# Sparse attention: the indexer's weighted sum on TensorE, the probabilities scaled on ScalarE, one rotation sum on GpSimd, and transfers traced by staging tile

## The chip, the cores and the metric

The kernel runs on one core of a Trainium2 chip. The metric is the device time of one execution in microseconds (us), as a median of runs. Engines are named as in the profile: PE is TensorE (PEld its weight loads), DVE is VectorE, ACT is ScalarE, POOL is GpSimd and SP is SyncE, whose queue starts the transfers.

## The reference, cut to what matters

A stack of six stages works on one sequence of 256 tokens with 1024 features: a state-space mixer (s5), an MLP (mlp0), sparse attention (dsa), an MLP (mlp1), a mixer of state-space and windowed attention (mix2) and a gated MLP (ffn2). Each stage but s5 is a few large products with weight matrices that are read from memory once. The change touches the sparse attention and the end of s5, and how the weights are fetched everywhere. The attention, shortened:

```
proj = h @ w_in
q, k, v, qi, ki, wi = split(proj); q, k, qi, ki = apply_rope(...)
wi = wi * (IDX_HEADS ** -0.5 * IDX_DIM ** -0.5)              # 8 indexer heads
rel = relu(einsum('bthd,bsd->bths', qi_blk, ki))
score = einsum('bths,bth->bts', rel, wi_blk)                 # sum over the 8 heads
score = where(causal, score, -inf)
_, idx = top_k(score, 64)
att = einsum('btngd,btknd->btngk', qg, kg) * scale           # only the chosen keys
p = softmax(where(valid, att, -inf))
o = einsum('btngk,btknd->btngd', p, vg)
out = o @ w_out
```

`apply_rope` is `x * cos + rot(x) * sin`: two products and a sum.

## The kernel before

All activations stay in SBUF in two halves of 128 tokens, h=0 and h=1. Every weight matrix is cut into units of 128 x 1024 fp32 (512 KB). `plan` writes down the order of all units of the whole kernel beforehand. `fetch` starts the transfer of a unit into a staging tile, `raw`, of which there are four. `send` calls `fetch` if that is still to be done and splits the unit into a high part `wh` (a cast on ACT, L162) and a low part `wl` (a subtraction shared by DVE and POOL, L165); the products then take three matmuls for each pair of operands (hi x hi, hi x lo, lo x hi, L223 and L233). `pump` calls `send` while there is a free pair of `wh` and `wl` tiles, `consumed` gives such a pair back. The splits have a lower priority than what is traced around them.

The order of the instructions on each engine is set when the program is built, by a scheduler that takes, of the instructions that it believes ready, the one traced first. On the chip each engine then works its list in order. The kernel helps with a clock of its own: `clock[0]` counts the estimated time of PE, `after(delay, fn)` puts a piece of work off, `tick` runs what is due, `need` forces it.

Stage s5 ends with a product of two halves (L710); `pump` is called just before it (L705), at a point with room for nine units (four in one pool, five in another). `fin(h, acc)` then normalises a half: squares on ACT (`act_squares`, L252), products with the gain on DVE (L309), a power on POOL (L257), the update of `x` (L312), and the same again for the next stage's norm (`pre_norm`), whose `dg` (L284) lets PE turn the half (L291) and start the next stage.

Stage dsa projects the indexer's columns and k, v for each half, then q in two chunks of heads. `idx_T` turns the indexer's queries and keys, `scores` multiplies them (L771), `rel` is the relu on ACT (L777), and DVE sums the eight heads with their weights `wis` (L784 for the first, L786 for seven more), 128 keys wide for h=0 and 256 for h=1. `topk` then runs eight rounds of max and replace on DVE and leaves `bias[h]`. `rope` runs on DVE (L718, L721, L722). `att(h, n)` treats four heads: scores (L867), masked scores with their maximum on DVE (L873), exponentials with their sum on ACT (L877), a reciprocal and the scaling of the four rows on DVE (L878, L880), then `turn_P` (transposes on PE, L887, copies on ACT, L890) and `pv` (L897). There are eight such calls; while they run, PE has the projection of q's second chunk and, once the heads are there, the product with `w_out` to do.

Of the kernel before, what the change touches and what calls it, by code (L numbers as in the profile page):

```python
# [11 lines left out]
F32 = mybir.dt.float32  # L12
# [30 lines left out]
INIT = 3  # L43
WARM = 12
# [6 lines left out]
def kernel(ctx: ExitStack, tc: tile.TileContext, d: dict, out: bass.AP, stages=None):  # L51
# [8 lines left out]
    raw_p = ctx.enter_context(tc.tile_pool(name="raw", bufs=4))  # L60
# [61 lines left out]
    stream = {"plan": [], "at": 0, "units": [], "sent": 0, "got": 0, "done": 0}  # L122
# [20 lines left out]

    def send():
        unit = stream["units"][stream["sent"]]
# [8 lines left out]
        raw = unit[6] if len(unit) > 6 else fetch(unit)  # L154
# [11 lines left out]
        unit[1:3] = [t[:, :tot].rearrange("p (k n) -> p k n", n=n) for t in (hi, lo)]  # L166

# [82 lines left out]
    def act_squares(src, ss, i, scale=1.0 / 32):  # L250
        junk = nrm_p.tile([128, 512], BF16, tag="junk", name="junk", bufs=1)
        act.activation(junk, src[:, HALVES[i]], AF.Square, scale=scale, accum_out=ss[:, i:i + 1])  # L252
# [50 lines left out]
    def post_norm(h, acc, gain):  # L303
        ss = square_sums()
        ag = nrm_p.tile([128, DM], F32, tag="xs", name="ag")
        for i in range(2):
            act_squares(acc, ss, i)
        for cs in HALVES:
            dve.tensor_tensor(ag[:, cs], acc[:, cs], gain[:, cs], OP.mult)  # L309
        r = rstd_of(ss)  # L310
        for cs in HALVES:
            dve.scalar_tensor_tensor(x[:, h, cs], ag[:, cs], r, x[:, h, cs], OP.mult, OP.add)  # L312

# [66 lines left out]
    def s5(hook):  # L380
# [290 lines left out]
        for i in range(8):  # L671
# [44 lines left out]
    def rope(dst, tmp, src, cos, sin, nh):  # L716
# [5 lines left out]
        dve.tensor_tensor(dst, dst, tmp, OP.add)  # L722
# [12 lines left out]
    def dsa(hook):  # L735
# [10 lines left out]
        pj = sp.tile([128, 2, 584], F32, name="pj")  # L746
        wis = sp.tile([128, 2, 8], F32, name="wis")
        qiT = sp.tile([128, 2, 4, 128], F32, name="qiT")
# [8 lines left out]
        def idx_T(h, io):  # L757
            iof = io.rearrange("p n e -> p (n e)")
            act.copy(qiT[:, h], transposes(iof[:, :512]).rearrange("p (j t) -> p j t", t=128))
# [3 lines left out]
            sco = rp.tile([128, T], F32, tag="sco", name="sco")[:, :nk]  # L763

            def scores(j0):
                need(*[ti[i] for i in range(h)])
                pss = [mm_tile().rearrange("p (j s) -> p j s", s=nk) for _ in range(2)]
                for j in range(j0, j0 + per):
                    for e in range(2):
                        es = slice(e * 64, e * 64 + 64)  # L770
                        pe.matmul(pss[e][:, j - j0, :], qiT[es, h, j, :], kiT[es, :nk], start=True, stop=True,  # L771
# [15 lines left out]

            def topk(j0):
                scores(j0)
                bs = base[:, T - nk:]  # L790
                dve.scalar_tensor_tensor(sco, bs, 1e30, sco, OP.add, OP.add)
# [7 lines left out]
            if h == 0:  # L799
                tix[h] = after(1.5, lambda: topk(0))  # L800
            else:
                def first():
                    scores(0)
                    tix[h] = after(2.0, lambda: topk(2))
                tix[h] = after(1.5, first)
# [8 lines left out]
        def on_kv(h, ps):  # L814
# [5 lines left out]
            tk[h] = after(4.0, lambda: act.copy(  # L820
# [4 lines left out]
        for h in range(2):  # L825
            need(xready[h])
            for n in range(2):
                ps = mm_tile()
                tok_mms(ps[:, :292], xTh, xTl, h, units[n])
                act.copy(pj[:, h, 292 * n:292 * n + 292], ps[:, :292])  # L830
            dve.tensor_scalar(wis[:, h], pj[:, h, 576:584], 8 ** -0.5 * 64 ** -0.5, None, OP.mult)
            io = rp.tile([128, 10, 64], F32, tag="S", name="io")
            it = rp.tile([128, 9, 64], F32, tag="rt", name="it", bufs=1)
            rope(io[:, :9], it, heads(pj[:, h, :576]), cosr[:, h], sinr[:, h], 9)
# [19 lines left out]
        def att(h, n):  # L854
# [24 lines left out]
            for i in range(4):  # L879
                dve.tensor_scalar(S[:, i], S[:, i], den[:, i:i + 1], None, OP.mult)  # L880
# [25 lines left out]
            fins[h, n] = after(3.2 + nk * 0.011, turn_P)  # L906
# [584 lines left out]
    def fin(h, acc):  # L1491
        name, nxt = now["name"], now["next"]
        with tc.high_priority(URGENT):
            if name in post_g:
                post_norm(h, acc, now["post"])
# [4 lines left out]
            else:  # L1500
                nc.sync.dma_start(out[0, HS[h], :], x[:, h, :])

# [97 lines left out]
```

## Time and profile before

| | |
|---|---|
| median of 3 runs | 1251.39 us (1243.54 to 1251.98) |
| the profiled execution | 1247.13 us, its span 1245.3 us |
| PE busy | 1203.2 us, 97% of the span |
| DVE, ACT, POOL busy | 859.4, 666.4, 362.2 us |

A busy PE is not PE at its full rate: the granted clock, the column PEclk, is 1.00 over most of the span and falls to about a half in a few places. Times in the trace are microseconds from the start of the span. dsa's products run from about 286 us to 411 us; s5 ends, and mlp0 begins, at about 99 us. Columns of a window are, for each engine, busy time and number of instructions.

### The profile page before, as it was taken

The numbers are of one execution on the slowest core, as the hardware profiler recorded it, in microseconds if no ns is written. First come the engines' busy times: TensorE is split into PE (matmuls) and PEld (weight loads), VectorE is DVE, ScalarE is ACT, GpSimd is POOL, SyncE is SP. The second block draws the span as 40 slices with busy tenths as digits, with TensorE's granted clock in tenths as the row PEclk, the third lists the DMA queues.
The fourth block names the chain that finished last, engine by engine and source line by source line (L and its number), as shares of the span: only waits on it lengthen the run. The fifth ranks groups of instructions, "written<-read, shape, count | busy, mean of one in ns | idle before, by whom it ended". The sixth has DMA issues, their size and how long they took to land.

```text
span 1245.3 us, 20243 instructions
## 1 busy us (share of the span) xinstructions
PE 1203.2 (97%) x7462; PEld 1031.5 (83%) x7462; DVE 859.4 (69%) x1560; ACT 666.4 (54%) x1207; POOL 362.2 (29%) x355
## 2 busy tenths in 40 slices
PE   7799999999889999999999999999999999999998
PEld 4347998988656899998889989988999888899997
DVE  7978654547986866553788875886776557797662
ACT  7636554436556655443555655665555344855541
POOL 6840000025311545441132124300111004655540
PEclk8899999999879999999999999999999999999999
DMA  8126655536430665552654465444443455766630
GB/s 332 35 81 205 202 188 187 201 113 197 158 125 4 217 202 192 178 193 85 208 164 151 136 195 178 132 143 137 121 134 110 147 170 178 250 194 208 180 108 34
DMA packets 107987, 198.51 MB, mean 159 GB/s; under 512 B 7569, under 2 KB 52593, under 8 KB 107889
## 3 DMA queue, kind: packets, MB, share of 16 engines
q1 hardware_dynamic: 107889, 197.23, 49.8%
q8 instruction: 59, 0.97, 0.3%
q14 instruction: 39, 0.32, 0.1%
HBM read 196.15 MB, written 1.05 MB: 158 GB/s over the span
## 4 chain that ended last, share of the span: by engine, by line
PE 71%; issue 7%; DVE 7%; DMA 4%; ACT 3%; POOL 2%; SPq 0%; DVEq 0%; ACTq 0%; POOLq 0%
PE mm L233 27%; PE acc L223 20%; PE mm L223 14%; DVE wl L165 2%; PE mm L263 1%; DMA raw<-in_w_up_dram 1%; POOL wl L165 1%; DMA raw<-in_mlp_w_dram 1%; DVE xbc L1056 1%; ACT wh L162 1%; PE mm L291 1%; PE mm L897 1%; PE acc L867 1%; PE mm L1117 1%; POOL rstd L257 1%
## 5 line engine op out<-in xcount | busy, mean ns | idle before, releaser
L165 DVE TENSOR_TENSOR wl<-raw,wh 128x512 fp32r<-128x512 f32 (+5 forms) x477 | 414.4, 904 | 183.8 <-ACT wh L162 173.8
L162 ACT CAST wh<-raw 128x512 fp32r<-128x512 f32 (+2 forms) x477 | 364.9, 814 | 212.6 <-PE acc L223 112.4
L165 POOL TENSOR_TENSOR wl<-raw,wh 128x96 fp32r<-128x96 f32 (+3 forms) x252 | 249.7, 1012 | 409.3 <-ACT wh L162 371.5
L233 PE MATMUL mm<-xTh,wh 128*128 128x256 f32 x1056 | 303.5, 287 | 0.0
L233 PE MATMUL mm<-xTh,wl 128*128 128x256 f32 x1056 | 298.8, 283 | 0.0
L233 PE MATMUL mm<-xTl,wh 128*128 128x256 f32 x1056 | 298.6, 283 | 0.0
L233 PEld LDWEIGHTS mm<-xTh,wh 128*128 128x128 f32 x1056 | 201.7, 191 | 4.3 <-issue 2.7
L233 PEld LDWEIGHTS mm<-xTl,wh 128*128 128x128 f32 x1056 | 201.9, 191 | 1.0
L233 PEld LDWEIGHTS mm<-xTh,wl 128*128 128x128 f32 x1056 | 201.8, 191 | 0.0
L223 PE MATMUL mm<-wh,xTh 128*128 128x512 f32 (+2 forms) x384 | 146.4, 386 | 0.0
L223 PE MATMUL mm<-wl,xTh 128*128 128x512 f32 (+2 forms) x384 | 142.8, 376 | 0.0
L223 PE MATMUL acc<-wh,hh 128*128 128x512 f32 x344 | 106.3, 390 | 0.0
L223 PE MATMUL acc<-wl,hh 128*128 128x512 f32 x344 | 106.2, 390 | 0.0
L223 PE MATMUL mm<-wh,xTl 128*128 128x512 f32 (+2 forms) x384 | 102.2, 381 | 0.8 <-DVE xTl L117 0.8
L223 PE MATMUL acc<-wh,hl 128*128 128x512 f32 x344 | 87.5, 390 | 0.0
L223 PEld LDWEIGHTS mm<-wh,xTh 128*128 128x128 f32 x384 | 73.1, 190 | 13.0 <-ACT xTh L116 0.3
L223 PEld LDWEIGHTS mm<-wl,xTh 128*128 128x128 f32 x384 | 73.0, 190 | 11.9
L223 PEld LDWEIGHTS mm<-wh,xTl 128*128 128x128 f32 x384 | 68.2, 190 | 13.7 <-issue 1.3
L223 PEld LDWEIGHTS acc<-wl,hh 128*128 128x128 f32 x344 | 64.6, 188 | 13.8
L223 PEld LDWEIGHTS acc<-wh,hl 128*128 128x128 f32 x344 | 64.4, 188 | 13.4
L223 PEld LDWEIGHTS acc<-wh,hh 128*128 128x128 f32 x344 | 63.2, 188 | 12.1
L257 POOL TENSOR_TENSOR rstd<-ss,mhalf 128x1 f32<-128x1 f32 x18 | 12.9, 719 | 182.2 <-DVE ss L255 177.5
(379 smaller groups left out, 1647.0 us busy)
## 6 DMA issues: line engine op xcount, KB each, us to landing
raw<-in_mlp_w_dram SPq DMA_DIRECT2D x128, 512.0 KB, 4.5
raw<-in_w_in_dram SPq DMA_DIRECT2D x69, 512.0 KB, 4.2
raw<-in_w_up_dram SPq DMA_DIRECT2D x36, 512.0 KB, 4.4
raw<-in_w_in_dram SPq DMA_DIRECT2D x64, 256.0 KB, 4.4
raw<-in_w_down_dram SPq DMA_DIRECT2D x22, 512.0 KB, 4.4
raw<-in_w_ssd_proj_dram SPq DMA_DIRECT2D x16, 512.0 KB, 3.7
raw<-in_att_w_in_dram SPq DMA_DIRECT2D x12, 512.0 KB, 4.9
gain<-in_norm_g_dram SPq DMA_DIRECT2D x9, 512.0 KB, 5.3
```

The source lines that it names most:

```text
L162: act.copy(hi[:, cs], raw[:, cs])
L165: eng.tensor_tensor(lo[:, cs], raw[:, cs], hi[:, cs].bitcast(F32), OP.subtract)
L223: pe.matmul(dst[:, a:b], half(lhs, k0 + k, h), rhs[:, a:b], start=first and i == 0 and rhs is wh and not lo, stop=last and i == len(units) ...
L233: pe.matmul(dst.rearrange("p (h t) -> p h t", h=2), lhs[:, c0:c0 + 128], rhs[:, :, k, :], start=i == 0 and m == 0, stop=i == len(units) - ...
L257: pool.tensor_tensor(r, ss[:, 0:1], mhalf[:, 0:1], OP.pow)
L263: pe.transpose(tp[:, j * 128:(j + 1) * 128], src[:, j * 128:(j + 1) * 128], ident)
L291: pe.matmul(tp[:, j * 128:(j + 1) * 128], xg[:, (a + j) * 128:(a + j + 1) * 128], dg, start=True, stop=True)
L867: pe.matmul(aps[:, e, j, :nk], qT[es, h, 2 * n + j, :], kT[es, n, :nk], start=True, stop=True, tile_position=(e * 64, 0))
L897: pe.matmul(ops[e * 64:e * 64 + 64, :256].rearrange("p (j t) -> p j t", j=2), kv[:, s, 256 + n * 64:256 + n * 64 + 64], PT[:, :, e, :], st ...
L1056: dve.scalar_tensor_tensor(o[:, s:], ps[:, e, :T - s], cwb[:, 3 - s, ft:ft + 1], o[:, s:], OP.mult, OP.add)
L1117: pe.matmul(ops[es, :128], v[:, s, g, c0:c0 + 64], PTs[e][:, b * 128:(b + 1) * 128], start=b == 0, stop=b == nb - 1, tile_position=(0, e * ...
```

## The change

Five things are changed, and three of them are in dsa.

1. The sum over the indexer's heads moves to PE. For each half POOL builds `dgw`, eight 128 x 128 diagonal matrices with the heads' weights (one instruction of 128 x 1024). The new `weigh` multiplies each head's `rel` by its diagonal and accumulates all eight in one PSUM tile, `tot`; `topk` reads that. `weigh` is put off by 2.5 us after the scores.
2. In `att` the four scalings move from DVE to ACT (Identity with a scale for each row), and `turn_P` is put off by 1.8 us more.
3. The sum in `rope` for q moves from DVE to POOL, and q's transposes are put off by 7 us instead of 6, k's by 5 instead of 4.
4. `prefetch` traces the transfers of up to four units beyond the last one sent, each time a unit is sent, instead of with the unit's own split. The number of staging tiles stays four.
5. At the end of s5 only six units are sent ahead of the last product; the rest is sent after the first half's squares, and its ACT instructions are queued behind them.

`pj` and `qiT` lose the copy that they had for each half, which makes room for `dgw`.

```
+RAWS = 4
+FIRST = 6
...
-        return raw
+
+    def prefetch():
+        while stream["asked"] < min(stream["sent"] + RAWS, len(stream["units"])):
+            fetch(stream["units"][stream["asked"]])
+            stream["asked"] += 1
 
     def send():
+        prefetch()
         unit = stream["units"][stream["sent"]]
...
-        raw = unit[6] if len(unit) > 6 else fetch(unit)
+        raw = unit[6]
...
         unit[1:3] = [t[:, :tot].rearrange("p (k n) -> p k n", n=n) for t in (hi, lo)]
+        prefetch()
...
-                for unit in stream["units"][:4]:
-                    fetch(unit)
+                prefetch()
...
-        pump()
+        while stream["sent"] < FIRST:
+            send()
         for h in range(2):
...
-            fin(h, acc)
+            squared = fin(h, acc)
+            if h == 0:
+                with tc.issue_after(squared.ins):
+                    pump()
...
-    def rope(dst, tmp, src, cos, sin, nh):
+    def rope(dst, tmp, src, cos, sin, nh, adder=None):
...
-        dve.tensor_tensor(dst, dst, tmp, OP.add)
+        (adder or dve).tensor_tensor(dst, dst, tmp, OP.add)
...
+            dgw = rp.tile([128, 8, 128], F32, tag="dgw", name="dgw", bufs=1)
+            pool.tensor_tensor(dgw, ident[:, None, :].to_broadcast([128, 8, 128]),
+                               wis[:, h, :, None].to_broadcast([128, 8, 128]), OP.mult)
+            tot = []
...
+                tix[h] = after(2.5, lambda: weigh(j0, rels))
+
+            def weigh(j0, rels):
+                if not tot:
+                    tot.append(mm_tile()[:, :nk])
                 for j in range(j0, j0 + per):
                     for e in range(2):
                         hd = 2 * j + e
-                        w = wis[:, h, hd:hd + 1]
-                        if hd == 0:
-                            dve.tensor_scalar(sco, rels[e][:, j - j0], w, None, OP.mult)
-                        else:
-                            dve.scalar_tensor_tensor(sco, rels[e][:, j - j0], w, sco, OP.mult, OP.add)
+                        pe.matmul(tot[0], dgw[:, hd], rels[e][:, j - j0], start=hd == 0, stop=hd == 7)
+                clock[0] += per * 2 * nk * 0.00086
+                if j0 + per < 4:
+                    scores(j0 + per)
+                else:
+                    topk()
...
-                dve.scalar_tensor_tensor(sco, bs, 1e30, sco, OP.add, OP.add)
+                dve.scalar_tensor_tensor(sco, bs, 1e30, tot[0], OP.add, OP.add)
...
-            tk[h] = after(4.0, lambda: act.copy(
+            tk[h] = after(5.0, lambda: act.copy(
...
-                rope(qr, qt, heads(ps), cosr[:, h], sinr[:, h], 8)
-                tq[h, n] = after(6.0, lambda: act.copy(
+                rope(qr, qt, heads(ps), cosr[:, h], sinr[:, h], 8, pool)
+                tq[h, n] = after(7.0, lambda: act.copy(
...
-                dve.tensor_scalar(S[:, i], S[:, i], den[:, i:i + 1], None, OP.mult)
+                act.activation(S[:, i], S[:, i], AF.Identity, scale=den[:, i:i + 1])
...
-            fins[h, n] = after(3.2 + nk * 0.011, turn_P)
+            fins[h, n] = after(5.0 + nk * 0.011, turn_P)
```

## Rows read from the trace of the kernel before

**Rows 1.** The page, busy time of each engine over the span.

```profile
PE 1203.2 (97%) x7462; PEld 1031.5 (83%) x7462; DVE 859.4 (69%) x1560; ACT 666.4 (54%) x1207; POOL 362.2 (29%) x355
```

**Rows 2.** Waits of PE, whole span: total us, times, longest us.

```profile
PE mm L291 <- DVE dg L284: 8.2, 5, 3.1
...
PE mm L263 <- ACT kr L819: 3.7, 1, 3.7
...
PE mm L887 <- DVE S L880: 2.7, 3, 2.1
```

**Rows 3.** Windows of 5 us: PE, PEld, DVE, ACT, POOL, clock, DMA share, GB/s.

```profile
95.00:100.00 5.00, 1.94 (x13) 1.22 (x11) 4.56 (x10) 3.85 (x12) 0.93 (x1) 1.00 0.31 86
100.00:105.00 5.00, 5.00 (x20) 4.25 (x19) 4.36 (x8) 3.64 (x7) 0.93 (x1) 0.66 0.70 213
...
300.00:305.00 5.00, 5.00 (x36) 4.66 (x35) 3.08 (x8) 1.82 (x4) 0.00 (x0) 1.00 0.27 99
...
320.00:325.00 5.00, 2.31 (x12) 1.36 (x10) 5.00 (x14) 1.68 (x3) 2.04 (x2) 1.00 0.32 102
325.00:330.00 5.00, 3.70 (x12) 2.75 (x14) 4.93 (x16) 2.49 (x5) 1.27 (x1) 0.54 0.67 234
330.00:335.00 5.00, 5.00 (x24) 3.25 (x20) 4.27 (x15) 1.08 (x2) 0.00 (x0) 0.78 0.53 195
...
350.00:355.00 5.00, 2.91 (x14) 2.11 (x12) 5.00 (x19) 3.72 (x12) 1.99 (x4) 1.00 0.26 91
355.00:360.00 5.00, 3.19 (x13) 1.55 (x13) 4.30 (x18) 3.82 (x13) 1.51 (x4) 0.61 0.10 22
360.00:365.00 5.00, 4.39 (x20) 2.91 (x22) 3.71 (x16) 1.82 (x4) 0.78 (x2) 0.50 0.58 188
365.00:370.00 5.00, 5.00 (x20) 3.00 (x17) 3.53 (x18) 2.92 (x13) 0.00 (x0) 0.52 0.03 5
```

**Rows 4.** Timeline of DVE, 310 to 320 us: start, us, instruction, count.

```profile
310.42 0.90 DVE L784 TENSOR_SCALAR sco<-rel,wis 128x128 f32<-128x128 f32 x1
...
316.92 0.99 DVE L786 SCALAR_TENSOR_TENSOR sco<-rel,wis,sco 128x128 f32<-128x128 f32 x1
...
319.97 1.27 DVE L722 TENSOR_TENSOR io<-io,it 128x576 f32<-128x576 f32 x1
```

**Rows 5.** Timeline of ACT, the copy of k and v, h=1.

```profile
322.43 0.58 ACT L815 COPY kv<-mm 128x512 f32<-128x512 f32 x1
```

**Rows 6.** Groups of DVE and ACT: count, busy us, mean ns.

```profile
L786 DVE SCALAR_TENSOR_TENSOR sco<-rel,wis,sco 128x128 f32<-128x128 f32 x7 | 4.2, 604 | 0.2
...
L786 DVE SCALAR_TENSOR_TENSOR sco<-rel,wis,sco 128x256 f32<-128x256 f32 x7 | 4.1, 579 | 0.4 <-ACT rel L777 0.3
...
L784 DVE TENSOR_SCALAR sco<-rel,wis 128x128 f32<-128x128 f32 (+1 forms) x2 | 1.3, 628 | 0.6 <-ACT rel L777 0.6
...
L722 DVE TENSOR_TENSOR qr<-qr,qt 128x512 f32<-128x512 f32 x4 | 2.7, 680 | 0.0
...
L880 DVE TENSOR_SCALAR S<-S,den 128x128 f32<-128x128 f32 (+1 forms) x32 | 8.8, 336 | 0.1
...
L877 ACT ACTIVATE S<-S,mx 128x128 f32<-128x128 f32 (+1 forms) x32 | 14.2, 448 | 2.2 <-DVE mx L875 2.2
```

**Rows 7.** Prices on PE and POOL: a timeline's two PE rows, a POOL group.

```profile
299.60 2.02 PE L291 MATMUL mm<-dg,xs 128*128 128x128 f32 x16 [2.32 <-DVE dg L284]
...
71.58 1.89 PE L668 MATMUL acc<-u,slot_wh 128*128 128x256 f32 x8
...
L640 POOL TENSOR_TENSOR r<-r,cos 128x512 f32<-128x512 f32 x8 | 10.2, 1274 | 8.2 <-DVE r L638 8.2
```

**Rows 8.** Timeline of s5's end, after the first half's product.

```profile
92.85 1.14 ACT L162 CAST wh<-raw 128x512 fp32r<-128x512 f32 x2 [1.22 <-DMA raw<-in_mlp_w_dram]
...
94.11 1.41 DVE L312 SCALAR_TENSOR_TENSOR x<-ag,rstd,x 128x512 f32<-128x512 f32 x2
```

**Rows 9.** Waits of SP's queue: total us, times, longest us.

```profile
SPq L140 <- DVE wl L165: 716.7, 283, 40.9
```

More of the change, by code (lines that the diff above doesn't have):

```diff
@@ L59 @@
     sm_p = ctx.enter_context(tc.tile_pool(name="sm", bufs=4))
-    raw_p = ctx.enter_context(tc.tile_pool(name="raw", bufs=4))
+    raw_p = ctx.enter_context(tc.tile_pool(name="raw", bufs=RAWS))
     w_p = ctx.enter_context(tc.tile_pool(name="w", bufs=8))
@@ L121 @@
     more_w = {"pool": None, "cap": MORE, "n": 0}
-    stream = {"plan": [], "at": 0, "units": [], "sent": 0, "got": 0, "done": 0}
+    stream = {"plan": [], "at": 0, "units": [], "sent": 0, "got": 0, "done": 0, "asked": 0}
     def room():
@@ L306, in post_norm @@
         for i in range(2):
-            act_squares(acc, ss, i)
+            squared = act_squares(acc, ss, i)
         for cs in HALVES:
@@ L312, in post_norm @@
             dve.scalar_tensor_tensor(x[:, h, cs], ag[:, cs], r, x[:, h, cs], OP.mult, OP.add)
+        return squared
     def add_x(h, acc, scale=None):
@@ L745, in dsa @@
         load(base, d["c_base"])
-        pj = sp.tile([128, 2, 584], F32, name="pj")
         wis = sp.tile([128, 2, 8], F32, name="wis")
-        qiT = sp.tile([128, 2, 4, 128], F32, name="qiT")
+        qiT = sp.tile([128, 4, 128], F32, name="qiT")
         kiT = sp.tile([128, T], F32, name="kiT")
@@ L758, in idx_T @@
             iof = io.rearrange("p n e -> p (n e)")
-            act.copy(qiT[:, h], transposes(iof[:, :512]).rearrange("p (j t) -> p j t", t=128))
+            act.copy(qiT, transposes(iof[:, :512]).rearrange("p (j t) -> p j t", t=128))
             act.copy(kiT[:, HS[h]], transposes(iof[:, 512:640], 1)[:, :128])
@@ L770, in scores @@
                         es = slice(e * 64, e * 64 + 64)
-                        pe.matmul(pss[e][:, j - j0, :], qiT[es, h, j, :], kiT[es, :nk], start=True, stop=True,
+                        pe.matmul(pss[e][:, j - j0, :], qiT[es, j, :], kiT[es, :nk], start=True, stop=True,
                                   tile_position=(e * 64, 0))
@@ L781, in scores, with topk @@
                         hd = 2 * j + e
-                        w = wis[:, h, hd:hd + 1]
-                        if hd == 0:
-                            dve.tensor_scalar(sco, rels[e][:, j - j0], w, None, OP.mult)
-                        else:
-                            dve.scalar_tensor_tensor(sco, rels[e][:, j - j0], w, sco, OP.mult, OP.add)
-            def topk(j0):
-                scores(j0)
+                        pe.matmul(tot[0], dgw[:, hd], rels[e][:, j - j0], start=hd == 0, stop=hd == 7)
[4 more added lines that the diff above has]
+                    topk()
+            def topk():
                 bs = base[:, T - nk:]
-                dve.scalar_tensor_tensor(sco, bs, 1e30, sco, OP.add, OP.add)
+                dve.scalar_tensor_tensor(sco, bs, 1e30, tot[0], OP.add, OP.add)
                 m8 = rp.tile([128, 8], F32, tag="m8", name="m8")
@@ L797, in topk @@
                 dve.tensor_tensor(bias[h], sco, bs, OP.add)
[L799 to L805, printed above, removed]
+            tix[h] = after(1.5, lambda: scores(0))
         def tok_chunk(c0, fn):
@@ L826, in dsa @@
             need(xready[h])
+            pj = rp.tile([128, 584], F32, tag="pj", name="pj", bufs=1)
             for n in range(2):
@@ L829, in dsa @@
                 tok_mms(ps[:, :292], xTh, xTl, h, units[n])
-                act.copy(pj[:, h, 292 * n:292 * n + 292], ps[:, :292])
-            dve.tensor_scalar(wis[:, h], pj[:, h, 576:584], 8 ** -0.5 * 64 ** -0.5, None, OP.mult)
+                act.copy(pj[:, 292 * n:292 * n + 292], ps[:, :292])
+            dve.tensor_scalar(wis[:, h], pj[:, 576:584], 8 ** -0.5 * 64 ** -0.5, None, OP.mult)
             io = rp.tile([128, 10, 64], F32, tag="S", name="io")
             it = rp.tile([128, 9, 64], F32, tag="rt", name="it", bufs=1)
-            rope(io[:, :9], it, heads(pj[:, h, :576]), cosr[:, h], sinr[:, h], 9)
+            rope(io[:, :9], it, heads(pj[:, :576]), cosr[:, h], sinr[:, h], 9)
             act.copy(io[:, 9], io[:, 8])
@@ L1492, in fin @@
         name, nxt = now["name"], now["next"]
+        squared = None
         with tc.high_priority(URGENT):
             if name in post_g:
-                post_norm(h, acc, now["post"])
+                squared = post_norm(h, acc, now["post"])
             else:
@@ L1501, in fin @@
                 nc.sync.dma_start(out[0, HS[h], :], x[:, h, :])
+        return squared
     def hook():
```

2 lines of the change are left out of this document (1 added, 1 removed).

## The prediction

> **What bounds the kernel now.** I read the page's busy times first: PE is busy for 1203.2 us, 97% of the span [rows 1]. So nearly everything that the other engines do is hidden, and what is taken off them is worth something only where PE stands still or runs at half its clock. The list of PE's waits came second [rows 2]: none of them is for weights, and the long ones are norms (`dg`), the rotation of k (`kr`, 3.7 us at once) and the scaled probabilities (`S` from L880). Two of these three lie in dsa. Third came windows of 5 us [rows 3], which show where and add the clock. What a window loses is its idle time and, of its busy time, the share by which the granted clock is under 1.00.
>
> Between 320 and 335 us PE idles 2.69 and 1.30 us and loses 3.70 x 0.46 + 5.00 x 0.22 = 2.8 us to the clock, together 6.8 us. Between 350 and 370 us it idles 2.09 + 1.81 + 0.61 = 4.5 us and loses 3.19 x 0.39 + 4.39 x 0.50 + 5.00 x 0.48 = 5.8 us, together 10.3 us. From 95 to 105 us, at the end of s5, it idles 3.06 us and loses 5.00 x 0.34 = 1.7 us, together 4.8 us. The first two places make 17.1 us in dsa; the same rows show DVE at 5.00 of 5 us in both where they begin. That is the queue that PE waits for.
>
> **Why DVE is late at 320 us.** The head sum for h=0 holds DVE from 310.42 to 317.9 us, splits in between; only then come the rotation of the indexer's second half, whose sum ends at 321.2 [rows 4], and the ACT copies that are queued behind it, the one of k and v at 322.43 [rows 5]. The rotation of k follows, and PE waits for it. The sum thus stands first in the chain that ends in the first loss.
>
> **The change, part by part.** *Head sum.* DVE loses 8 instructions for each half: 4.2 + 4.1 us for the fourteen fused ones and 1.3 us for the two first ones, 9.6 us [rows 6]. PE gains eight fp32 matmuls for each half, each two instructions in this trace. For 128 keys the nearest row is the turn L291: 16 instructions in 2.02 us; for 256 keys it is L668: 8 in 1.89 us, so 16 in 3.8 us [rows 7]. That is 5.8 us on PE at the full clock; below nothing it can't go, since the work is new, and at half the clock it is 11.6 us. All of it lies on the path, because PE has other work ready nearly everywhere. POOL gains two `dgw` of 1024 columns; L640 does 512 in 1.27 us [rows 7], so some 2.5 us each. Its cover is the wait between `wis` and the scores, over 8 us for each half by the kernel's own clock; if POOL is late, PE waits in order, with every later product behind it.
>
> *q's rotation sum.* Four times 0.68 us leave DVE [rows 6], and four times about 1.27 us go to POOL [rows 7]. Splits on POOL queue behind them, and they behind splits; the transposes are put off by 1 us to cover the difference.
>
> *Scaling.* 32 instructions leave DVE, 8.8 us; the nearest ACT row, the exponentials over the same tiles, has 14.2 us for 32 [rows 6]. An exponential is no cheaper than a plain scaling, so I take 14.2 us as the upper end and the 8.8 us of DVE as the lower. In 350 to 370 us ACT is busy 12.3 of 20 us [rows 3], and half of the calls, 4 to 7 us, would fall there. It fits, but with little room. Behind each scaling on ACT stand the copies of transposed tiles for which PE waits.
>
> *What comes back.* Up to 362 us DVE loses 9.6 us, three rotation sums (2.0 us) and two calls' scalings (2.2 us), 13.8 us of some 50. The first loss is one delay of 3.7 us that follows from a sum of 7.5 us in the way, so I count all 6.8 us as recovered. In the second, the heads of h=0 are treated with no dense product left beside them but that of the output; earlier probabilities let that begin earlier, but ACT has more to do. Its ends are 0 and 10.3 us; I take half, 5.1 us. dsa gives 6.8 + 5.1 - 5.8 = 6.1 us.
>
> *End of s5.* The normalisation of the first half shares ACT and DVE with splits: a cast waits 1.22 us for a transfer at 92.85 us, and the update of x behind its split starts at 94.11 [rows 8]. With the later units queued behind the squares it can start some 1.4 us earlier, and the same kind of cast between the next squares costs 0.6 us more. PE's idle 3.06 us [rows 3] shrink by 1.4 to 2.0 us. The clock may then stay up: after an idle time of 2.32 us at 297 to 299.60 [rows 7] the window from 300 us shows 1.00 [rows 3], against 0.66 after 3.06 us. So 1.4 us without and 3.7 us with the clock; I take 2.5. Six units are sent beforehand, and the eight of the first two chunks are needed over the first 11 us of mlp0, so the weights should hold out; if not, PE waits for a cast and a split, about 1.5 us.
>
> *Prefetch by staging tile.* SP's queue waited 716.7 us in 283 waits for splits that free a staging tile [rows 9]. Transfers already start when a tile is free; tracing them earlier gives no more tiles. What can change is the order between weights and the few small loads. I count nothing, with ends of -2 and +2 us. Putting the transposes and `turn_P` off costs nothing as long as PE has ready work to fill in.
>
> **The sum.** 6.1 + 2.5 = 8.6 us. On the profiled execution that makes 1247.1 - 8.6 = 1238.5 us. That execution lies 4.3 us under the median of the runs, 1251.4, within their spread of 8.4 us; for the median I forecast 1251.4 - 8.6 = 1243 us. One per cent is 12.5 us, about what a measurement of this kernel can tell from no change.
>
> **The rivals.** *All of it comes back.* If both losses of dsa vanish and the clock holds at s5's end, the gain is 17.1 - 5.8 + 3.7 = 15 us: 1236 us. For it speaks that DVE is full in both places, against it that the second stretch is a chain of five engines, which is not shortened by one of them.
>
> *ACT takes DVE's place.* If the scalings fill ACT between 350 and 370 us, the second loss stays whole: 6.8 - 5.8 + 2.5 = 3.5 us, 1248 us. ACT's row there speaks for it, its idle 7.7 us against.
>
> *POOL blocks DVE, and the time goes back.* DVE's sum for 128 keys took 604 ns, that for twice the columns 579 [rows 6]: at 310 to 318 us POOL is splitting beside it, later it is not. POOL gets 2 x 2.5 + 4 x 1.27 = 10.1 us more, against 13.8 us that DVE loses up to 362 us. If each of these instructions held up a DVE instruction as long, DVE would gain next to nothing, and PE would wait as before, with its new 5.8 us on top and a `dgw` for which it waits in order. That is +5.8 - 2.5 = +3.3 us, and with the new matmuls at half the clock +9.1 us: 1255 to 1260 us. It decides from the point where POOL finishes `dgw` after the relu. Against it: DVE's rounds of max and replace have one operand in SBUF, and the kernel's masked scores one in PSUM. The Trainium skill, "SBUF — State Buffer", section "Who interferes with whom", says that a DVE instruction with two SBUF inputs and a GpSimd instruction that reads SBUF exclude each other for a whole instruction. By that rule the splits and k's rotation would be the ones held up; the 604 against 579 ns agree with it.
>
> *The prefetch does nothing.* It is in the forecast already.
>
> **How the numbers follow.** Chances: the forecast 0.50, all comes back 0.17, ACT takes its place 0.20, POOL blocks 0.13. The forecast's own ends, 0 to 10.3 us for the second loss, 1.4 to 3.7 us for s5 and 2 us either way for the transfers, give 1235 to 1251 us. The range from 1230 to 1257 us takes in the first two rivals with the runs' own spread below, and the lower half of the third. Faster than 1238.9 us are most of the second case and a tenth to a fifth of the first: 0.25. Slower than 1263.9 us needs the third rival and more: 0.06. The rest, 0.69, is within 1%.
>
> **What the profile after would show.** Right: no wait of several us for `kr`, the windows from 320 to 335 us at a clock of 1.00, `dg` after s5's first half earlier by 1.4 us or more, 32 more instructions on ACT at 0.3 to 0.45 us. Wrong: waits of PE for `dgw` or `rel`, ACT full beside an idle PE, transposes of q that wait for POOL, or the long wait moved to another line with the clock down as before. The order on each engine is set when the program is built, so a badly placed instruction that is late on the chip is what would upset this forecast most.

## The result, and the profile after

The change makes the kernel a little slower: 1254.84 us (1251.73 to 1258.5, 20 runs) against 1247.88 us (1243.33 to 1254.04, 20 runs), a ratio of 1.0060 with a 95% interval of 1.0046 to 1.0073. That is 7.5 us at 1247 us. The forecast was a gain of 8.6 us, so the sign is wrong, and the time lies near the upper end of the range. The profiled execution took 1258.5 us, its span 1256.7 us; it is the longest of the twenty, 3.7 us over their median.

The page's line of busy times, as [rows 1]: DVE lost 12 us, and PE gained 11.5.

```profile
PE 1214.7 (97%) x7494; PEld 1041.3 (83%) x7494; DVE 847.1 (67%) x1508; ACT 677.5 (54%) x1239; POOL 378.3 (30%) x361
```

PE's waits, as [rows 2]. The norms' `dg` grew from 8.2 to 10.4 us, the wait for `kr` is still there, and that for the scaled `S` has gone to ACT and grown.

```profile
PE mm L299 <- DVE dg L292: 10.4, 5, 3.8
...
PE mm L902 <- ACT S L895: 3.9, 3, 2.1
PE mm L271 <- ACT kr L833: 3.3, 1, 3.3
```

The windows, as [rows 3]; columns as there. The stages lie later, so the places are read by what happens in them: 300 to 310 us is dsa's entry, 330 to 340 the wait for `kr`, 360 to 385 the heads.

```profile
300.00:305.00 5.00, 1.57 (x7) 1.44 (x7) 4.49 (x8) 0.23 (x1) 2.92 (x2) 0.84 0.93 317
305.00:310.00 5.00, 5.00 (x28) 4.66 (x28) 1.74 (x4) 2.01 (x4) 0.00 (x0) 0.82 0.03 11
...
330.00:335.00 5.00, 1.67 (x9) 1.13 (x10) 4.91 (x18) 2.69 (x5) 0.87 (x1) 0.91 0.84 300
335.00:340.00 5.00, 5.00 (x20) 3.61 (x19) 1.87 (x5) 1.08 (x2) 0.71 (x1) 0.75 0.38 121
...
360.00:365.00 5.00, 2.78 (x15) 1.82 (x14) 3.94 (x10) 4.32 (x16) 2.19 (x2) 0.98 0.00 0
365.00:370.00 5.00, 3.13 (x20) 2.08 (x20) 4.98 (x17) 4.34 (x15) 2.53 (x4) 0.50 0.01 3
370.00:375.00 5.00, 4.30 (x16) 2.49 (x18) 2.97 (x17) 4.75 (x16) 1.64 (x3) 0.50 0.67 219
375.00:380.00 5.00, 4.58 (x18) 2.71 (x16) 1.67 (x11) 3.82 (x15) 0.00 (x0) 0.65 0.62 200
380.00:385.00 5.00, 4.34 (x16) 3.03 (x17) 3.26 (x21) 4.34 (x16) 0.00 (x0) 0.69 0.00 0
```

By the forecast's own measure (idle time, and busy time by what the clock is under 1.00) the entry loses 3.43 + 1.15 = 4.6 us, where [rows 7] show an idle 2.32 us and [rows 3] a full clock. The wait for `kr` loses 3.33 + 1.4 = 4.7 us (6.8 before), and the heads 5.9 + 6.7 = 12.6 us (10.3 before). What was to vanish has moved and stayed.

The entry is where the first new thing stands. DVE's timeline there, then POOL's and PE's:

```profile
300.34 0.75 DVE L730 TENSOR_TENSOR io<-pj,cosr 128x576 f32<-128x576 f32 x1
301.53 1.91 DVE L292 TENSOR_SCALAR dg<-ident,rstd 128x128 f32<-128x128 f32 x1 [0.44 <-POOL rstd L265]
```

```profile
300.44 1.05 POOL L265 TENSOR_TENSOR rstd<-ss,mhalf 128x1 f32<-128x1 f32 x1 [2.87 <-DVE wis L846]
301.47 1.89 POOL L776 TENSOR_TENSOR dgw<-ident,wis 128x1024 f32<-128x1024 f32 x1
311.67 1.58 POOL L172 TENSOR_TENSOR wl<-raw,wh 128x320 fp32r<-128x320 f32 x1 [8.31 <-ACT wh L169]
```

```profile
303.59 3.55 PE L299 MATMUL mm<-dg,xs 128*128 128x128 f32 x16 [3.43 <-DVE dg L292]
```

`dg` waits for `rstd` from POOL, and POOL has `dgw` next in its list: it starts that 0.06 us before DVE starts `dg`. `dg` now ends 0.08 us after `dgw`, 1.91 us after it began. Behind this `dgw` POOL stands idle for 8.31 us, so that at the entry only DVE is held up and no split is late by it. In the kernel before, the `dg` at this place took 0.29 us with POOL idle. The `dg` of dsa's first half took 0.90 us there, beside the first of three splits on POOL, so the trace of the kernel before already held the sign:

```profile
281.13 3.19 POOL L165 TENSOR_TENSOR wl<-raw,wh 128x320 fp32r<-128x320 f32 x3
...
281.20 0.90 DVE L284 TENSOR_SCALAR dg<-ident,rstd 128x128 f32<-128x128 f32 x1 [0.73 <-POOL rstd L257]
...
299.17 0.29 DVE L284 TENSOR_SCALAR dg<-ident,rstd 128x128 f32<-128x128 f32 x1 [0.44 <-POOL rstd L257]
```

PE, which waits for `dg`, then turns the half in 3.55 us instead of the 2.02 of [rows 7], at a granted clock of 0.84 and 0.82 in the two windows, between the levels of 1.2 and 2.4 GHz. For the second half the same pair stands in front of k's rotation:

```profile
321.29 1.88 DVE L733 TENSOR_TENSOR it<-pj,sinr 128x288 f32<-128x288 f32 x1
...
323.30 0.92 DVE L733 TENSOR_TENSOR it<-pj,sinr 128x288 f32<-128x288 f32 x1
...
330.75 0.40 DVE L730 TENSOR_TENSOR kr<-kv,cosr 128x256 f32<-128x256 f32 x1
```

```profile
320.61 2.25 POOL L776 TENSOR_TENSOR dgw<-ident,wis 128x1024 f32<-128x1024 f32 x1 [0.20 <-DVE wis L846]
322.82 3.50 POOL L172 TENSOR_TENSOR wl<-raw,wh 128x320 fp32r<-128x320 f32 x3
```

Beside `dgw`, and then beside the splits that queued up behind it, the two products of the rotation take 1.88 and 0.92 us; the mean of the four before was 0.447 us:

```profile
L721 DVE TENSOR_TENSOR it<-pj,sinr 128x288 f32<-128x288 f32 x4 | 1.7, 447 | 0.0
```

### The profile page after: what moved, and what is told of

Read it like the earlier page. It is cut to its first block, busy times and chain, and to the rows that moved or that the text cites. A ratio compares the mean times of both kernels' runs of the same rounds, so it can differ in the third digit from the quotient of the medians.

```text
span 1256.7 us, 20291 instructions
## 1 busy us (share of the span) xinstructions
PE 1214.7 (97%) x7494; PEld 1041.3 (83%) x7494; DVE 847.1 (67%) x1508; ACT 677.5 (54%) x1239; POOL 378.3 (30%) x361
## 3 DMA queue, kind: packets, MB, share of 16 engines
HBM read 196.15 MB, written 1.05 MB: 157 GB/s over the span
## 4 chain that ended last, share of the span: by engine, by line
PE 51%; issue 6%; DVE 3%; ACT 2%; DMA 2%; POOL 1%; SPq 0%; DVEq 0%; ACTq 0%; POOLq 0%
PE mm L241 22%; PE acc L231 12%; PE mm L231 11%; DMA raw<-in_w_up_dram 1%; DVE xbc L1071 1%; PE mm L271 1%; ACT wh L169 1%; DVE wl L172 1%; PE mm L1132 1%; POOL wl L172 1%; ACT P L1112 0%; PE mm L1294 0%; PE mm L1260 0%; DMA raw<-in_w_down_dram 0%; DMA raw<-in_w_in_dram 0%
## 5 line engine op out<-in xcount | busy, mean ns | idle before, releaser
L172 POOL TENSOR_TENSOR wl<-raw,wh 128x96 fp32r<-128x96 f32 (+3 forms) x252 | 256.4, 1038 | 395.9 <-ACT wh L169 343.0
```

Source lines behind the costliest of these rows:

```text
L172: eng.tensor_tensor(lo[:, cs], raw[:, cs], hi[:, cs].bitcast(F32), OP.subtract)
```

## The experiments

In the table, dsa is the time from its first turn on PE (`mm<-dg`) to the next stage's first turn, read from PE's timeline of one execution. The kernel before has 282.6 to 407.0, 124.4 us; the changed one 285.5 to 418.4, 132.9 us. All ratios are to the kernel before, on the same chip; each run has 5 to 12 executions.

| run | what runs | median us | ratio, 95% | dsa us |
|---|---|---|---|---|
| e1_headsum | before + part 1 | 1251.62 | 1.0031 (1.0016 to 1.0047) | 130.4 |
| e2_scale | before + part 2 | 1247.19 | 0.9985 (0.9969 to 1.0000) | 124.9 |
| e3_rope | before + part 3 | 1248.61 | 1.0008 (0.9993 to 1.0023) | 123.5 |
| e4_fetchtail | before + parts 4, 5 | 1247.00 | 0.9988 (0.9973 to 1.0003) | 121.2 |
| e8_245 | before + parts 2, 4, 5 | 1247.57 | 0.9995 (0.9978 to 1.0011) | 122.6 |
| e12_no_headsum | after without part 1 | 1250.08 | 1.0010 (0.9996 to 1.0025) | 123.7 |
| e6_no_scale | after without part 2 | 1254.24 | 1.0057 (1.0037 to 1.0078) | 132.2 |
| e15_no_rope | after without part 3 | 1252.93 | 1.0049 (1.0032 to 1.0065) | 131.1 |
| e16_parts_123 | after without parts 4, 5 | 1256.92 | 1.0074 (1.0052 to 1.0096) | 131.4 |
| e13_no_sum | before, 13 of 16 sum steps left out | 1240.86 | 0.9957 (0.9942 to 0.9972) | 117.5 |
| e14_weigh_twice | after, products of the sum twice | 1261.34 | 1.0117 (1.0101 to 1.0133) | 139.1 |
| e11_weigh_bf16 | after, the sum in bf16 | 1252.84 | 1.0039 (1.0020 to 1.0058) | 128.0 |
| e5_dgorder | after, `wis` behind `dg` | 1254.62 | 1.0062 (1.0040 to 1.0084) | 131.7 |
| e7_kvprio | before, k's rotation first | 1248.50 | 1.0012 (0.9997 to 1.0026) | 128.1 |
| e9_k_later | before, k's transposes later | 1247.63 | 0.9986 (0.9971 to 1.0000) | 125.6 |
| e10_k_later_after | after, k's transposes later | 1253.03 | 1.0040 (1.0026 to 1.0053) | 128.2 |
| e17_diag_act | after, diagonals on ACT | 1248.22 | 0.9998 (0.9985 to 1.0011) | 123.5 |
| e18_45_k_later | before + parts 4, 5, k later | 1246.04 | 0.9981 (0.9965 to 0.9997) | 125.4 |

### Which part it is

The edits are the parts of the diff ahead of the prediction, one or several at a time.

> The kernel before with the head sum on PE alone (diagonals from POOL, accumulation on PE, one copy of pj and qiT). Theory 1, the new work on PE and the diagonal's instruction on POOL beside the norm's dg on DVE are the loss: 4 to 8 us slower than before, dg for dsa's second half takes well over 1 us instead of 0.3, and the second turn into dsa comes 2 to 4 us later. Rival, ACT's scalings are the loss: within 2 us of before, since the stall for kr that it removes pays for the 5.8 us on PE.

> The kernel before with the four scalings of each attention call on ACT alone and turn_P put off by 1.8 us more. Theory 1: within 2 us of before. Rival, ACT becomes the queue that PE waits for: 3 to 7 us slower, ACT busy over 4 of 5 us from the first attention call to the end of the last, PE waits for S from the scaling on ACT.

> The kernel before with q's rotation sum on POOL alone, and the transposes of q and k put off by 1 us more. Both theories: within 2 us of before; if POOL's instructions hold up DVE's splits, up to 3 us slower.

> The kernel before with the transfers traced by staging tile and the new order at the end of s5, without any change in dsa. Theory 1: 0 to 2 us slower, since a cast that waits for a transfer now stands between the two squares of the first half; the turn into mlp0 then comes 0.5 to 1 us later. If the tail does what I forecast: 1.5 to 3.5 us faster.

> The kernel before with the scaling on ACT, the early transfers and the new order at the end of s5, without the head sum on PE and without the rotation sum on GpSimd. If parts that were harmless alone add up: 1.2 + 1.8 us or so faster than before, 1243 to 1246 us. If their gains were noise or share one place: within 1 us of before, 1247 to 1248 us. Theory that the loss of the whole change hangs on the head sum: in any case not slower than before.

> The changed kernel with the head sum back on DVE; scaling on ACT, q's rotation sum on GpSimd, early transfers and the new end of s5 stay. Theory (the whole loss hangs on the head sum): within 2 us of the kernel before, 1245 to 1249 us, and dsa takes 121 to 125 us from its first turn to the next stage's, against 130 and more in each kernel with the head sum. Rival (each part costs a little, and the sum of the four left is 3 us or more): 1250 us and over.

> The changed kernel without part 3: the rotation sum of q is back on DVE with the old delays. Theory (GpSimd's rotation sum is late together with the head sum, since every rotation then waits behind GpSimd's splits and diagonals): 2.5 to 4 us faster than the changed kernel, near the head sum alone, 1251 to 1252 us. Rival (the rest is the scaling or the early transfers together with the head sum): within 1.5 us of the changed kernel, 1253.5 to 1256 us.

> The kernel before with the three parts in dsa alone (head sum on PE, scaling on ACT, rotation sum on GpSimd), without the early transfers and the new end of s5. If the 3 us come from the parts in dsa together: as the whole change or slower, 1254 to 1257 us. If they come from the transfers and the end of s5: near the head sum alone, 1251 to 1252.5 us.

Of these, each kernel with the head sum on PE is slower by 0.3% or more, and its dsa takes 130 us or longer; without it none is slower by more than the interval can tell, and dsa takes 121 to 125 us. So most of the loss, at the least, hangs on part 1. Alone it costs 3.9 us, with the others 7.5 us, though the others cost nothing by themselves (-1.9, +1.0 and -1.5 us). All of them together, e12_no_headsum, cost 1.2 us by the ratio, with no change inside its interval; its median of 1250.08 us just reaches the rival's 1250, so that a cost of up to 3 us isn't excluded. The small gains don't add up: e8_245 is within 1 us of the kernel before. Taking out part 3, or parts 4 and 5, gives 1.0049 and 1.0074; both intervals overlap that of the whole change. So these runs don't say which of them makes the head sum dearer.

The rival that ACT takes DVE's place was tried by taking part 2 out.

> The changed kernel with the scaling of the probabilities back on DVE and the old delay of the transposes. Theory A (ACT takes DVE's place: with the head sum on PE the heads of both halves come closer together, and the scalings fill ACT between 360 and 385 us, where it was busy 4.3 to 4.8 of each 5 us): ACT falls back to under 4 us in each window there, the clock is under 0.7 for less time, and the kernel is 3 to 5 us faster than the changed one. Rival B (PE's own new work and the late rotation of k set the delay, ACT's load is only where PE has nothing to do anyway): within 1 us of the changed kernel.

ACT's load did fall, as two windows of the heads in this run show (with the scalings it was 4.34 and 4.75 of 5 us, above):

```profile
365.00:370.00 5.00, 3.56 (x17) 2.05 (x17) 4.72 (x11) 3.13 (x12) 2.06 (x4) 0.50 0.64 213
370.00:375.00 5.00, 5.00 (x26) 3.18 (x24) 3.30 (x21) 2.04 (x8) 0.00 (x0) 0.50 0.33 105
```

The clock is at a half all the same, and the time, 1254.24 us, is that of the changed kernel. ACT was full, but nothing hung on that: rival B.

### What the head sum is worth on DVE, and what it costs on PE

```
-                        else:
+                        elif hd == 2 * j0:
                             dve.scalar_tensor_tensor(sco, rels[e][:, j - j0], w, sco, ...)
```

> The kernel before with 13 of the 16 instructions of the head sum on DVE left out (one is kept for each pass of scores, so the keys are chosen by a part of the heads). PE has no new work. Theory A, the prediction's step (the sum stands first in the chain that ends in the two losses of dsa): idle time and clock loss there shrink by up to 12 us, 7 to 12 us faster than before, 1235 to 1240 us. Theory B (the sum is beside the path: PE's wait for the rotation of k and the heads' chain are set by PE's order and by chains that start later): within 2 us of before, 1245 to 1248 us, with the wait for kr still 3 us or more.

5.4 us faster, between the two theories. The wait for `kr` is there as B said, but the clock holds behind it:

```profile
325.04 0.66 PE L263 MATMUL mm<-ident,kr 128*128 128x128 f32 x4 [2.98 <-ACT kr L819]
```

```profile
320.00:325.00 5.00, 2.06 (x12) 1.41 (x10) 5.00 (x15) 1.96 (x4) 1.78 (x2) 1.00 0.46 161
325.00:330.00 5.00, 4.60 (x24) 3.36 (x25) 3.24 (x6) 3.27 (x6) 1.56 (x1) 1.00 0.77 277
```

The first loss falls from 6.8 to 3.3 us. So what taking this sum off DVE can give is some 5.4 us (3.5 to 7.2 by the interval, with three of the sixteen steps still in). Then PE's side:

```
+                        for twice in range(2):
+                            pe.matmul(tot[0], dgw[:, hd], rels[e][:, j - j0],
+                                      start=hd + twice == 0, stop=hd + twice == 8)
```

> The changed kernel with each product of the head sum issued twice into the same sum, which doubles every score and leaves the choice of keys as it was. PE gets 5.7 us more (1.9 + 3.8 us by the rows of the changed kernel). Theory (the new products lie on the path and are paid in full): 5 to 7 us slower than the changed kernel, 1260 to 1262 us. Rival (they fill time in which PE would stand still, and the loss is delay): under 3 us slower, 1255 to 1257 us.

```
-            dgw = rp.tile([128, 8, 128], F32, ...)
+            dgw = rp.tile([128, 8, 128], BF16, ...)
...
-                    rel = rp.tile([128, per, nk], F32, ...)
+                    rel = rp.tile([128, per, nk], BF16, ...)
```

> The changed kernel with the relu's output and the diagonals of the head sum kept in bf16, so that each product of the head sum is one pass of PE; the sum is rounded, so the choice of keys can differ from the reference's. Theory (the loss is PE's new work, paid in full at 5.8 us as the two rows of 1.95 and twice 1.89 us say, and nothing comes back for it): the head sum takes 1.5 us or so of PE instead of 5.8, and the kernel is 3 to 4.5 us faster than the changed one, 1250.5 to 1252 us. Rival (the loss is delay, the weighing being late in a chain, or GpSimd's diagonals in DVE's way): PE's part shrinks and the time stays within 1.5 us of the changed kernel, 1253.5 to 1256 us.

The groups of these products in the changed kernel and in the one with bf16 (count, busy us, mean ns):

```profile
L802 PE MATMUL mm<-rel,dgw 128*128 128x256 f32 x16 | 3.8, 379 | 0.0
...
L802 PE MATMUL mm<-rel,dgw 128*128 128x128 f32 x16 | 1.9, 275 | 0.0
```

```profile
L802 PE MATMUL mm<-rel,dgw 128*128 128x256 bf16 x8 | 1.2, 274 | 0.0
...
L802 PE MATMUL mm<-rel,dgw 128*128 128x128 bf16 x8 | 0.6, 221 | 0.0
```

A second set of products made the kernel slower by 1.0117 - 1.0060, 7.1 us, for 5.2 us more of busy time in its trace (7.2 + 3.7 us in place of 3.8 + 1.9): they are paid in full. In bf16 3.9 us of busy time are gone and 2.6 us came back (1.0060 - 1.0039), between the theories; the intervals of these two ratios overlap, so this gain by itself is not clear of noise. Scaled to 5.7 us of busy time it gives 3.8 us, so the price of the products is put at 4 to 7 us. By this reckoning even a head sum on PE that held up nobody would only break even: 5.4 us from DVE, about 5.7 us to PE. The missing 7 us are something else.

### What else the head sum does

The order on DVE at the entry was altered first: `wis` waits for `dg`, so that POOL can't start `dgw` sooner.

```
+            with tc.issue_after(last_dg[0].ins):
                 dve.tensor_scalar(wis[:, h], pj[:, 576:584], 8 ** -0.5 * 64 ** -0.5, None, OP.mult)
```

> The changed kernel with one order altered: DVE works the second half's heads' weights (wis) only after the norm's dg of that half, so POOL's diagonals (dgw), which need wis, no longer run while DVE builds dg. Theory (POOL's 1024-column dgw holds up a DVE instruction for its whole time, and at dsa's entry that is the dg for which PE waits): the dg takes 0.3 us instead of 1.9, the second turn of dsa starts 1.6 us earlier or more, the clock stays up at 300 to 305 us, and the kernel is 1.6 to 3.5 us faster than the changed one, 1251 to 1253 us. Rival (the entry is long because the first half's weighing and rotation sit in front of PE's turn in the order, whatever DVE does): dg gets short and the second turn does not move, 0 us.

DVE's timeline in this run, and POOL's:

```profile
298.43 0.28 DVE L292 TENSOR_SCALAR dg<-ident,rstd 128x128 f32<-128x128 f32 x1 [0.44 <-POOL rstd L265]
298.63 0.16 DVE L848 TENSOR_SCALAR wis<-pj 128x8 f32<-128x8 f32 x1
299.48 2.04 DVE L734 TENSOR_TENSOR it<-pj,sinr 128x288 f32<-128x288 f32 x2 [0.68 <-DMA sinr<-in_c_sin_dram]
```

```profile
298.94 1.90 POOL L777 TENSOR_TENSOR dgw<-ident,wis 128x1024 f32<-128x1024 f32 x1 [0.55 <-DVE wis L848]
```

`dg` is back at 0.28 us, and `dgw` now holds up the rotation behind it: 2.04 us for two products that take 0.81 us where nothing is beside them. The second half is as it was (1.89 and 0.92 us, and a wait of 3.9 us for `kr`). The entry got shorter by 0.6 us, from 18.1 to 17.5 us between the two turns, and the time didn't move. By itself this looked like the rival's win: that the place of `dgw` doesn't matter. It only shows that moving the collision doesn't remove it. e11_weigh_bf16 shows it in a third place: there `dgw` ran beside the product that stands before `dg` in DVE's list. That took 2.39 us instead of 0.75, `dg` was short (0.27 us) but late, and PE waited 3.58 us for it.

```profile
298.38 1.90 POOL L776 TENSOR_TENSOR dgw<-ident,wis 128x1024 bf16<-128x1024 f32 x1
...
298.50 2.39 DVE L730 TENSOR_TENSOR io<-pj,cosr 128x576 f32<-128x576 f32 x1 [0.65 <-DMA cosr<-in_c_cos_dram]
```

Next, PE's wait for `kr`, from two sides: k's rotation at high priority on DVE and ACT, and k's transposes later in PE's list.

```
+            with tc.high_priority(URGENT):
                 act.copy(kv[:, h], ps)
                 ...
                 act.copy(kr[:, :, 1, :], kr[:, :, 0, :])
```

> The kernel before, with the copies of k and v and the rotation of k traced at high priority, so that DVE and ACT work them ahead of the splits that are queued there; PE's order stays as it was. Theory (PE's wait for the rotation of k at 330 us comes from the static order on DVE, splits and rounds of max and replace placed ahead of it, and not from how much DVE has to do): the wait of 3.7 us for kr vanishes, the clock stays up from 325 to 335 us, 3 to 6 us faster than before, 1241 to 1245 us. Rival (DVE is full there, so that what is moved ahead delays the weights' splits by as much and PE waits for those): within 1 us of before, with waits for wl or wh in place of kr.

```
-            tk[h] = after(4.0, lambda: act.copy(
+            tk[h] = after(9.0, lambda: act.copy(
```

> The kernel before with one number changed: the transposes of the rotated k are put off by 9 us instead of 4, so that PE's list has some 15 more products of q (about 4 us) ahead of the second half's. Theory (the wait of 3.7 us is set by PE's own order: PE reaches the transposes one microsecond after the product of k and v is done, and copy, rotation and copy take 3 us and more whatever DVE was doing before): the wait for kr is gone, idle time plus clock loss between 320 and 335 us falls from 6.8 to under 3 us, dsa takes 3 to 5 us less (120 to 121 us from its first turn to the next stage's), and the kernel is 2 to 5 us faster than before, 1242 to 1245 us. Rival (what PE does earlier here is missing later, between 350 and 370 us, where it waits for the heads): the wait goes and the time stays within 1 us of before.

> The changed kernel with the same: the transposes of the rotated k are put off by 9 us instead of 5. Theory (as for the kernel before; the head sum on PE left this wait as it was, 3.3 us, because it is set by PE's order): the wait is gone and the kernel is 2 to 5 us faster than the changed one, 1250 to 1252 us, still slower than before by the new products. Rival: the wait moves to 350 to 380 us, 1254 to 1255 us.

With high priority the wait is 3.3 instead of 3.7 us and the time the same, without the waits for weights that the rival named. With the later transposes the wait for `kr` is gone, and two others stand in its place. PE's timeline of e9_k_later:

```profile
328.36 2.56 PE L771 MATMUL mm<-kiT,qiT 64*128 64x256 f32 x8 [1.90 <-ACT rel L777]
...
333.38 1.08 PE L263 MATMUL mm<-ident,kr 128*128 128x128 f32 x4 [2.46 <-DVE qt L721]
```

The gain is 1.7 us in the kernel before, where no change is still at the end of the interval, and 2.5 us in the changed one. In the kernel before, the loss between 320 and 335 us is 6.4 us by the forecast's measure, against 6.8 before and the under 3 us that were expected. I read the wait as a place where PE runs ahead of DVE, not as one instruction that is late.

Last, POOL. ACT builds the diagonals; PE's order in dsa is unchanged.

```
-            pool.tensor_tensor(dgw, ident[:, None, :].to_broadcast([128, 8, 128]),
-                               wis[:, h, :, None].to_broadcast([128, 8, 128]), OP.mult)
+            for hd in range(8):
+                act.activation(dgw[:, hd], ident, AF.Identity, scale=wis[:, h, hd:hd + 1])
```

> The changed kernel with the diagonals dgw built by ACT, eight scalings of 128x128 for each half, in place of one GpSimd instruction; PE's order in dsa is unchanged. Theory (GpSimd's dgw holds up the DVE instruction beside it for its whole time, the dg at dsa's entry by 1.6 us and the rotation of the second half by 1.4 + 0.5 us): dg takes 0.3 us, the two products of the rotation 0.45 us each, dsa 2 to 4 us shorter, and the kernel is 2 to 4 us faster than the changed one, 1251 to 1253 us. Rival (the delay is in the order: PE's turn and the rotation wait for other work anyway): within 1 us of the changed kernel, 1254 to 1256 us, or slower by what ACT gets.

1248.22 us, more than the theory asked for: 0.9998 against 1.0060, 7.7 us faster than the changed kernel. The profiled execution is the shortest of its twelve, 1244.59 us, so the sizes in the trace are to be read with that in mind. DVE's rows for the same three instructions, then PE's two that waited for them, then the windows of the entry and of the wait for `kr`:

```profile
296.83 0.28 DVE L292 TENSOR_SCALAR dg<-ident,rstd 128x128 f32<-128x128 f32 x1
...
313.42 0.86 DVE L733 TENSOR_TENSOR it<-pj,sinr 128x288 f32<-128x288 f32 x1
...
314.41 0.43 DVE L733 TENSOR_TENSOR it<-pj,sinr 128x288 f32<-128x288 f32 x1
```

```profile
297.26 2.02 PE L299 MATMUL mm<-dg,xs 128*128 128x128 f32 x16 [1.10 <-DVE dg L292]
...
323.92 0.66 PE L271 MATMUL mm<-ident,kr 128*128 128x128 f32 x4 [1.56 <-ACT kr L833]
```

```profile
300.00:305.00 5.00, 5.00 (x37) 4.79 (x37) 3.44 (x7) 3.43 (x8) 1.19 (x1) 1.00 0.06 25
...
320.00:325.00 5.00, 3.44 (x21) 2.51 (x21) 5.00 (x16) 2.50 (x5) 2.27 (x2) 1.00 0.71 210
325.00:330.00 5.00, 5.00 (x28) 3.96 (x24) 2.56 (x8) 1.28 (x3) 1.27 (x1) 1.00 0.64 215
```

PE stands still for 1.10 us at the entry instead of 3.43, and for 1.56 us at `kr` instead of 3.33, and the clock stays at 1.00 in both places, so that the turn takes 2.02 us again. Of the 2.3 us by which the wait at the entry is shorter, 1.6 are `dg`; 0.5 are `rstd` ahead of it, 0.55 us here and 1.05 us in the changed kernel and in the kernel before. ACT pays 5.0 us for the 16 scalings, and PE waits for none of them. POOL also has 4.1 us less in its list. At the entry no split stood behind `dgw`; for the second half three did, and there the runs don't tell the delay of DVE from that of the splits.

The harmless edits were put together at the end.

> The kernel before with the early transfers, the new end of s5, and k's transposes put off by 9 us instead of 4; nothing of the head sum, the scaling or the rotation. Each was 1.5 to 1.7 us faster than before by itself, at the edge of what five rounds can tell. If they add up: 1243 to 1245 us, a ratio of 0.997 to 0.998. If both are chance: 1246 to 1248 us.

1246.04 us, 0.9981: 2.4 us faster than before, with an interval that just excludes no change. Of the versions that do the whole work it is the one whose interval lies below 1, and by no more than that.

## Why the prediction was wrong

**The step that failed** is the one on `dgw`: "Its cover is the wait between `wis` and the scores, over 8 us for each half". That was true for PE, which never waited for `dgw`, and it was the wrong question. I asked who waits for the new POOL instruction and not what DVE does while it runs. It stands right behind `rstd` in POOL's list, so it starts just when DVE starts the `dg` for which PE is waiting. The sum had this term at nothing. Taking the diagonals off POOL, at the same PE work and order, is worth 7.7 us, as much as the whole loss. From a gain of 8.6 us to a loss of 7.5 us the forecast missed by 16.1 us: about half is this term, and most of the rest is what was to come back, below. That the time still lies within 1230 to 1257 us is owed to the width of the range, and in part to its base: the three executions before the forecast have a median of 1251.4 us, the twenty of the result 1247.9 us.

**The rival "POOL blocks DVE"** had the mechanism and nearly the time (1255 to 1260 us, at a chance of 0.13), but not the place: I put it at 310 to 318 us, and had it decide where `dgw` is later than the relu, for which no run shows a sign. I also weighed it by the Trainium skill, "SBUF — State Buffer", section "Who interferes with whom", with half of the rule only: two SBUF inputs. The same section of the Trainium skill says that `tensor_scalar` and copies can enter, where their operands allow it, modes that take the ports that DVE shares with GpSimd, and that whoever issues first keeps the shared pair for the whole instruction. The rows agree with that half too: `dg` is a TENSOR_SCALAR, started 0.06 us after `dgw`, and ended with it, 1.91 us instead of 0.29. That it runs in such a mode no row shows.

**The head sum's price on PE**, 5.8 us, was right: 5.7 us busy, and doubling it costs 7.1 us. So was ACT's for the scalings, 11.9 us (6.8 + 5.1) between the 8.8 and 14.2 of the forecast.

**What comes back**, 6.8 + 5.1 us, was too much, apart from POOL. Leaving nearly all of DVE's sum out gives 5.4 us, not 11.9. (The 11.9 also counted the rotation sums and scalings that leave DVE; parts 2 and 3 alone give -1.9 and +1.0 us.) The forecast took a wait as recovered because the sum stood first in its chain. The wait for `kr` is still 2.98 us without the sum, and 3.6 us in e12_no_headsum; with the transposes at or near their old place only e17_diag_act has less, 1.56 us. Of the first loss 3.5 us go in e13_no_sum, 2.8 of them the clock. In the heads e13_no_sum loses 7.8 us by the same measure (its windows from 345 to 365 us) and e17_diag_act 9.7 (from 350 to 370), against 10.3: of the 5.1 us counted there, 2.5 came back without the sum and 0.6 in the whole change with its diagonals on ACT. That this chain of five engines is not shortened by one of them the text itself had said against the first rival.

**End of s5**, 2.5 us: not shown. The twelve profiled executions with part 5 begin mlp0's turn at 98.9 us on the mean (97.3 to 101.3), the eight without at 99.2 (97.9 to 101.3). In the changed kernel a cast waits 1.21 us for its transfer between the two squares, which start 2.41 us apart; in the kernel before, the cast between them didn't wait, and they started 1.09 us apart. So the chain there is no shorter:

```profile
91.05 0.59 ACT L260 ACTIVATE junk<-acc 128x512 bf16<-128x512 f32 x1
...
92.94 0.62 ACT L169 CAST wh<-raw 128x512 fp32r<-128x512 f32 x1 [1.21 <-DMA raw<-in_mlp_w_dram]
93.46 0.59 ACT L260 ACTIVATE junk<-acc 128x512 bf16<-128x512 f32 x1
```

Only the units after the sixth were moved behind the squares; this cast belongs to one of the six.

**Prefetch** at nothing, and **scaling on ACT** with room, were right: parts 4 and 5 alone give 0.9988, part 2 alone 0.9985, SP's queue still waits 723.8 us in 283 waits (716.7 in [rows 9]), and without part 2 the changed kernel isn't faster.

**The sum, in the measured prices:** -5.4 (DVE's sum) + 5.7 to 7.1 (PE's products) + 7.7 (POOL's diagonals) - 2.4 (the other parts alone, -1.9 + 1.0 - 1.5) = +5.6 to +7.0 us, against 7.5 measured. Each of these terms is uncertain by some 2 us. With the +1.2 us of e12_no_headsum, the other parts together, in place of the -2.4, the sum is +9.2 to +10.6 us, so it closes only within these uncertainties. Open is why the head sum alone costs 3.9 us and not the 8.0 to 9.4 of its own three terms. Its trace shows no cheaper diagonals: `dg` takes 1.91 us beside `dgw` there too, and PE's waits for `dg` (below) and for `kr` (4.8 us) are longer than in the changed kernel. The head sum alone with its diagonals on ACT wasn't tried, nor the diagonals on ACT together with the later transposes.

```profile
304.29 3.75 PE L291 MATMUL mm<-dg,xs 128*128 128x128 f32 x16 [4.26 <-DVE dg L284]
```

## What to carry to other kernels

Before work goes to an idle GpSimd, list what VectorE has in its queue at that moment, and ask which of it the busy engine waits for: the price is the VectorE instruction beside it, not the GpSimd instruction itself. Price a sum that is to be moved from a half-hidden engine to the full one by leaving it out first: here that gives 5.4 us, and the new products cost about as much. An edit that only reorders a collision proves nothing about it; put the work on a third engine to see its price.

## What was not expected of the hardware

One 128x1024 instruction on POOL (1.89 to 2.25 us) stretched a 128x128 TENSOR_SCALAR on DVE from 0.29 to 1.91 us, and a product of 128x288 from 0.45 to 1.88 us, so these took nearly as long as POOL did. A `dg` beside a split on POOL took 0.90 us in the kernel before the change, so this could have been read there.

The turn at dsa's entry took 3.45 to 3.75 us at a lowered clock in all nine profiles with the diagonals on POOL, but also in four of the eleven without. The length of PE's wait alone doesn't decide it: after 2.32 us [rows 7] the turn took 2.02 us, after 2.17 us in e2_scale 3.65 us. So the 1.5 us of slower work at the entry are not `dgw`'s alone.

```profile
298.48 3.65 PE L291 MATMUL mm<-dg,xs 128*128 128x128 f32 x16 [2.17 <-DVE dg L284]
```
